# First weights by input block, part of a modulation on TensorE, two matmuls of the last pair moved ahead of its recurrence, four output loads, and a new order of stages, in a two-layer encoder

## The chip, the cores and the metric

The kernel runs on one core of a Trainium2 chip. A core has TensorE (PE in the views; PEld is its loading of weights), VectorE (DVE), ScalarE (ACT), GpSimd (POOL) and SyncE (SP, whose queue issues most DMAs here). Each engine works through its own instructions in order and waits on semaphores for the others. The metric is the device time of one execution in microseconds; lower is better.

## The reference

The input x is 512 tokens of 1024 channels. Two layers, each a mixer and a gated ConvFFN, both as residual blocks with a conditioned RMS norm; then a final norm. The change is in the mixer of layer 0:

```
shift, scale, gate = split(silu(c) @ ada_w[0, 0] + ada_b[0, 0])      # 3 x 1024, one vector
h = rmsnorm(x, norm_g) * (1 + scale) + shift
p = h @ ab_w_in                      # 1024 -> 2560 (hgrn: q, f_fwd, f_bwd, i, g) + r, k, v, wd, ad, gd
y_a = hgrn2(...)                     # 4 heads of 128, both directions, chunks of 32
# rwkv: 8 heads of 64, both directions, in pairs of heads
g = sigmoid(gd) @ g2
for each direction:
    w = -softplus(-(w0 + tanh(wd) @ w2)) - 0.5;  decay = exp(-exp(w));  a = sigmoid(a0 + ad @ a2)
    k_d = k * (1 + (a - 1) * k_a)
    state = state * decay + (state a_t) b_t + v_t k_t;   y += state r_t
    bonus += sum(r * k_d * r_k, per head) * v
y_b = (groupnorm(y) * lnx_w + lnx_b + bonus) * g
x = x + gate * (concat(y_a, y_b) @ ab_w_out)
```

## The kernel before

Activations lie with channels on the 128 partitions and the 512 tokens along the free dimension, so x is eight tiles of 128x512 (an "input block" each). Weights come in blocks of 128x128. Every large product is done in three passes of reduced fp32: a tile is split into a high part (`hi`, by a cast on ACT) and a low part (`lo`, by a subtraction on DVE), and `mm3` issues hi x hi, hi x lo and lo x hi into one PSUM bank. `load_w` loads the blocks of one output block (512 KB for eight inputs) and makes both parts; `gemm` runs `mm3` over the input blocks. PSUM has banks by tag: g, m and c two each, h and o one each.

`start_in` is the first stage. It loads x, takes the norm, and computes shift and scale of this modulation: per input block b a load `ada0` of 1 MB (128 x 2 x 1024) and two dots on DVE (`dot`, L232), each over 1024 columns; then bias (L375), scale (L376) and `modulate` (L171 to L173: nt on DVE, the high half on ACT, the low half on DVE) give the split tile of h. The weights of six output blocks FIRST (k, wd, ad, r, v and gd, in the banks g c g c h o) are loaded one output block after another, 512 KB each, and their 144 matmuls follow.

Then layer 0 proper. Its work is cut into stages: for each of four pairs of rwkv heads `pair` (projections and elementwise preparation), `unit0` and `unit1` (one for each direction: the small triangular solves, a long chain of short DVE instructions at L641 and L643), `inv0` and `inv1` (`rwkv_inverse`, L706 to L735: solve results go through DRAM, loaded as Z and ZT, then TensorE steps at L706, L716, L727 and L733), `chain0` and `chain1` (`rwkv_chain`: a recurrence of 7 steps over chunks, then 16 output matmuls), `post` (`rwkv_post`: group norm, bonus, gate); for each of four hgrn heads `proj` and `hgrn`; and `gate`, `ada` (later modulations) and `out` (early part of the output projection). The list PLAN names each stage, its pair or head, and a number of priority; a scheduler takes from the ready instructions of each engine by priority, so PLAN decides the order in which the engines find the work. `tc.high_priority(...)` raises a piece of code above it.

`rwkv_post` of the last pair is the last work of the mixer: its end normalises the sum of both directions, transposes it, scales it (L781, L784 on ACT), adds the bonus (matmul of `kds` with a block matrix of ones, L788, then DVE L789 and L790) and multiplies by the gate (matmul `lg` x `gd`, L792, then DVE L793). `encoder` then loads the output weights of the two inputs that came last (`ab_out2`, two loads of 512 KB for four output blocks each), multiplies, adds to x (L1179, L334) and forms the next norm (L272). Layer 0's mixer ends at about 622 us of the span; the rest (a ConvFFN, layer 1, a ConvFFN, the final norm) is untouched.

Of the kernel before, what the change touches and what calls it, by code (L numbers as in the profile page):

```python
# [9 lines left out]
F32 = mybir.dt.float32  # L10
F32R = mybir.dt.float32r
# [5 lines left out]
P = 128  # L17
# [21 lines left out]
for _n, _k in COLS:  # L39
# [16 lines left out]
PLAN = [  # L56
    ("pair", 0, 18000), ("proj", 0, -900), ("unit0", 0, 2000), ("unit1", 0, -1000), ("pair", 1, -1000),
# [6 lines left out]
    ("proj", 2, 4500), ("ada", 1, 3200), ("hgrn", 2, 0), ("inv0", 3, 0), ("proj", 3, -5300),  # L64
    ("chain0", 3, 15000), ("inv1", 3, -1500), ("post", 2, 0), ("ada", 2, 1000), ("chain1", 3, 11100),
    ("out", 0, 1400), ("out", 1, -3500), ("hgrn", 3, 14000), ("post", 3, 0),
]
# [3 lines left out]
def encoder(ctx: ExitStack, tc: tile.TileContext, A, out, dbg=None):  # L71
# [272 lines left out]
    def start_in(pool, pool2):  # L344
# [20 lines left out]
        hs, ws = [], {}  # L365
        ps = {i: mps(tag=t) for i, t in zip(FIRST, "gcgcho")}
        for b in range(KB):
            raw = mk(pool, [P, 2, D], "ada", bufs=ADB)
            nc.sync.dma_start(raw, A["ada0"][b])
            if b < len(ps):  # L370
                ws[FIRST[b]] = load_w(A["ab_in"][FIRST[b]], KB, pool2, 2 * len(ps) - 2)
            with tc.high_priority(2 * URGENT):
                for i in range(2):
                    dot(raw[:, i], row, mod[:, b + 8 * i:b + 8 * i + 1])
                dve.tensor_tensor(mod[:, b:b + 9:8], mod[:, b:b + 9:8], col("ada_b", b, 9)[:, ::8], op=ALU.add)  # L375
                dve.scalar_tensor_tensor(gsc[:, b:b + 1], mod[:, 8 + b:9 + b], 1.0, col("norm_g", b), op0=ALU.add, op1=ALU.mult)  # L376
                t = mk(pool, [P, T], "nt", bufs=3)
                hs.append(modulate(t, x[b], rs, gsc[:, b:b + 1], mod[:, b:b + 1]))
        for i in FIRST:
            gemm(ps[i], ws[i], hs, KB)  # L380
        return hs, ps
# [63 lines left out]
    def layer0(ys):  # L445
# [314 lines left out]
        def rwkv_post(q):  # L760
# [17 lines left out]
            for j in range(4):  # L778
# [7 lines left out]
                           scale=col("rwkv_lnx_w", p)[64:128], bias=col("rwkv_lnx_b", p)[64:128])  # L786
            pb = mps(tag="o")
            pe.matmul(pb, bones, kds, start=True, stop=True)  # L788
            dve.tensor_tensor(kds, pb, v, op=ALU.mult)  # L789
            dve.tensor_tensor(y, y, kds, op=ALU.add)  # L790
            pg = mps(tag="o")
            pe.matmul(pg, lg, gd[0], start=True, stop=True)  # L792
            dve.tensor_tensor(y, y, pg, op=ALU.mult)  # L793
# [414 lines left out]
def _layout(inp):  # L1208
# [13 lines left out]
    a["ab_out1"] = np.stack([wo[:, :, list(ks)] for ks in EARLY])  # L1222
    a["ab_out2"] = wo[:, :, list(LATE)].reshape(2, 4, P, 2, P).transpose(0, 2, 1, 3, 4).reshape(2, P, 8, P)
    a["cd_in"] = blocks(f("cd_w_in")[0])[CD_ORDER]
# [45 lines left out]
```

## Time and profile before

| what | us |
| --- | --- |
| median of 3 runs | 1515.57 |
| the runs | 1512.7 to 1520.62 |
| profiled execution | 1522.82 |
| its span | 1521.0 |
| mean granted clock of TensorE in it | 0.944 of full |

Times of the views are those of the profiled execution, counted from the start of its span; the execution is a little longer than the span. A share of busy time is a mean over stages with different limits.

### The profile page before, as it was taken

The page shows a single profiled execution, that of the slowest core. Times are in us where ns is not written, and L with a number is a line of the kernel's source. Part 1 is how long each engine was busy: PE and PEld are TensorE (multiplying, and loading weights), DVE is VectorE, ACT ScalarE, POOL GpSimd, SP SyncE. Part 2 cuts the span into 40 slices and gives each one's busy share as a digit, 9 for nine tenths or more (in the row PEclk, how much of TensorE's full clock was granted, in tenths as well). Part 3 has the DMA queues.
Part 4 walks back from the last instruction along what each step waited for, and adds up shares of the span by engine and source line. Part 5 has one row for each costly group of instructions (what it writes and reads, how often), then busy time and mean ns, then how long its engine had stood idle before and what let it go on. Part 6 is the DMA issues. An engine that isn't in the chain of part 4 may idle for free.

```text
span 1521.0 us, 22382 instructions
## 1 busy us (share of the span) xinstructions
PE 1412.9 (93%) x8446; PEld 1117.7 (73%) x8446; DVE 1028.0 (68%) x2119; ACT 682.8 (45%) x1221; POOL 148.3 (10%) x217
## 2 busy tenths in 40 slices
PE   5997879889998997999999999999999999999997
PEld 3765557566766674788888888887688888888886
DVE  7679776878787864766555795579878654544544
ACT  4454543645544542643233233477465432332343
POOL 1030201102110000000000000039600000000000
PEclk7998688999999996999999999999999999999998
DMA  9221122332252540444644683232133332223221
GB/s 372 74 76 47 50 58 71 102 94 65 65 183 62 177 136 19 165 162 142 202 145 135 227 334 88 96 108 63 35 105 119 117 97 98 94 87 111 94 73 56
DMA packets 77005, 175.08 MB, mean 115 GB/s; under 512 B 28257, under 2 KB 34273, under 8 KB 75873
## 3 DMA queue, kind: packets, MB, share of 16 engines
q1 hardware_dynamic: 76896, 173.65, 35.3%
q8 instruction: 66, 1.08, 0.3%
q14 instruction: 43, 0.34, 0.1%
HBM read 166.80 MB, written 6.82 MB: 114 GB/s over the span
## 4 chain that ended last, share of the span: by engine, by line
PE 72%; DVE 14%; ACT 5%; issue 4%; DMA 3%; POOL 2%; SPq 1%; DVEq 0%; POOLq 0%; ACTq 0%
PE g L144 9%; PE g L146 8%; PE g L145 8%; PE c L145 6%; PE c L144 6%; PE c L146 6%; PE o L144 3%; PE o L145 3%; PE o L146 3%; PE h L144 3%; PE h L146 3%; PE h L145 3%; DVE wlo L139 2%; PE c L733 2%; DVE tt L641 1%
## 5 line engine op out<-in xcount | busy, mean ns | idle before, releaser
L138 ACT CAST whi<-raw 128x512 fp32r<-128x512 f32 (+1 forms) x402 | 242.8, 609 | 520.4 <-PE g L145 204.7
L139 DVE TENSOR_TENSOR wlo<-raw,whi 128x512 fp32r<-128x512 f32 (+1 forms) x402 | 280.5, 703 | 188.7 <-ACT whi L138 185.3
L144 PE MATMUL g<-h,whi 128*128 128x512 f32 x586 | 243.2, 415 | 15.9 <-ACT h L172 5.1
L146 PE MATMUL g<-h,wlo 128*128 128x512 f32 x586 | 237.2, 405 | 4.3 <-DVE wlo L139 4.3
L145 PE MATMUL g<-h,whi 128*128 128x512 f32 x586 | 238.6, 407 | 2.8 <-DVE h L173 2.8
L144 PEld LDWEIGHTS g<-h,whi 128*128 128x128 f32 x586 | 114.3, 195 | 47.5 <-ACT h L172 6.4
L146 PEld LDWEIGHTS g<-h,wlo 128*128 128x128 f32 x586 | 114.3, 195 | 32.6 <-DVE wlo L139 5.9
L145 PEld LDWEIGHTS g<-h,whi 128*128 128x128 f32 x586 | 114.5, 195 | 29.8 <-DVE h L173 4.0
L144 PE MATMUL c<-h,whi 128*128 128x512 f32 x306 | 122.1, 399 | 0.0
L145 PE MATMUL c<-h,whi 128*128 128x512 f32 x306 | 121.2, 396 | 0.0
L146 PE MATMUL c<-h,wlo 128*128 128x512 f32 x306 | 120.6, 394 | 0.0
L1108 POOL TENSOR_TENSOR cpa<-cpa,ta 128x512 f32<-128x512 f32 x51 | 73.5, 1460 | 1.9
L232 DVE SCALAR_TENSOR_TENSOR ra<-ra,row 128x1024 f32<-128x1024 f32 x56 | 67.9, 1218 | 0.0
L144 PEld LDWEIGHTS c<-h,whi 128*128 128x128 f32 x306 | 58.5, 191 | 12.8 <-ACT whi L138 0.3
L145 PEld LDWEIGHTS c<-h,whi 128*128 128x128 f32 x306 | 58.8, 192 | 12.3 <-issue 0.5
L146 PEld LDWEIGHTS c<-h,wlo 128*128 128x128 f32 x306 | 58.5, 191 | 12.0
L641 DVE TENSOR_TENSOR tt<-L,xi 128x60 f32<-128x60 f32 (+24 forms) x248 | 55.7, 225 | 16.7 <-DMA L<-nd 11.3
L643 DVE TENSOR_TENSOR xi<-xi,tt 128x60 f32<-128x60 f32 (+24 forms) x248 | 54.4, 219 | 5.4
L746 ACT COPY X<-c 64x64 f32<-64x64 f32 x56 | 11.7, 208 | 84.0 <-DVE X L745 83.5
L144 PE MATMUL o<-h,whi 128*128 128x512 f32 x122 | 48.1, 394 | 0.8 <-DVE ot L793 0.8
L145 PE MATMUL o<-h,whi 128*128 128x512 f32 x122 | 47.9, 393 | 0.0
L146 PE MATMUL o<-h,wlo 128*128 128x512 f32 x122 | 47.9, 393 | 0.0
(437 smaller groups left out, 2906.5 us busy)
## 6 DMA issues: line engine op xcount, KB each, us to landing
raw<-ffn_up SPq DMA_DIRECT2D x88, 512.0 KB, 3.4
ra<-ada SPq DMA_DIRECT2D x56, 512.0 KB, 4.2
raw<-ab_in SPq DMA_DIRECT2D x35, 512.0 KB, 3.6
raw<-ffn_down SPq DMA_DIRECT2D x32, 448.0 KB, 3.3
raw<-ada SPq DMA_DIRECT2D x24, 512.0 KB, 4.1
ada<-ada SPq DMA_DIRECT2D x8, 1024.0 KB, 10.7
raw<-ffn_down SPq DMA_DIRECT2D x16, 512.0 KB, 3.6
raw<-cd_in SPq DMA_DIRECT2D x12, 512.0 KB, 3.3
```

The lines of the kernel that those rows point to most:

```text
L138: act.copy(hi[:, :n, :], raw[:, k0:k0 + n, :])
L139: dve.tensor_tensor(lo[:, :n, :], raw[:, k0:k0 + n, :], hi[:, :n, :].bitcast(F32), op=ALU.subtract)
L144: pe.matmul(ps, whi, xhi, start=first, stop=False)
L145: pe.matmul(ps, whi, xlo, start=False, stop=False)
L146: pe.matmul(ps, wlo, xhi, start=False, stop=last)
L232: dve.scalar_tensor_tensor(w, w, 1.0, row, op0=ALU.mult, op1=ALU.mult, accum_out=dst)
L641: dve.tensor_tensor(tv, Lv[:, j + 1:, j:j + 1].broadcast_to([P, n, m]), xi[:, j:j + 1, :m].broadcast_to([P, n, m]), op=ALU.mult)
L643: dve.tensor_tensor(xi[:, j + 1:, :m], xi[:, j + 1:, :m], tv, op=ALU.add)
L733: pe.matmul(ps[h][:, c, :], W[hr, c0 + c, :], BRS[hr, c0 + c, :], start=True, stop=True)
L746: act.copy(X[64:128, 1, cn], ps[64:128])
L1108: pl.tensor_tensor(pa, pa, tp, op=ALU.add)
```

## The change

1. **Start.** The modulation of input blocks 0, 1, 3 and 5 (`BY_PE`) is done on TensorE: 32 matmuls of 128x32 with silu(c) as stationary operand, on 64 columns each, then one DVE transpose of 128x64. Blocks 2, 4, 6 and 7 keep the dots. The weights of the six FIRST outputs come by input block (128 x 6 x 128, 384 KB, three buffers) with one cast and one subtraction of 768 columns, and the 18 matmuls of an input block stand right behind its modulation.
2. **Last pair.** The bonus matmul and its multiplication, and the gate matmul with an ACT copy into the space of k, stand ahead of the recurrence of the second direction. `rwkv_post` then only adds and multiplies.
3. **Last output weights.** Four loads of 256 KB (two outputs each); three are issued inside the layer's block of pools, ahead of its end, and none takes the second pool.
4. **PLAN** has a new order and new numbers.

```diff
-    ("pair", 0, 18000), ("proj", 0, -900), ("unit0", 0, 2000), ("unit1", 0, -1000), ("pair", 1, -1000),
+    ("pair", 0, 19000), ("proj", 0, -3500), ("unit0", 0, 5000), ("unit1", 0, -1000), ("inv0", 0, 3000),
...
             raw = mk(pool, [P, 2 * D], "ada", bufs=ADB)
             nc.sync.dma_start(raw, A["ada0"][b])
-            if b < len(ps):
-                ws[FIRST[b]] = load_w(A["ab_in"][FIRST[b]], KB, pool2, 2 * len(ps) - 2)
+            wraw = mk(pool, [P, len(FIRST), P], "wraw", bufs=3)
+            nc.sync.dma_start(wraw, A["ab_first"][b])
             with tc.high_priority(2 * URGENT):
-                for i in range(2):
-                    dot(raw[:, i], row, mod[:, b + 8 * i:b + 8 * i + 1])
-                dve.tensor_tensor(mod[:, b:b + 9:8], mod[:, b:b + 9:8], col("ada_b", b, 9)[:, ::8], op=ALU.add)
+                if b in BY_PE:
+                    v = raw.rearrange("p (k q i) -> p k q i", k=KB, q=4)
+                    pa = mps([P, 64])
+                    for k in range(KB):
+                        for q in range(4):
+                            pe.matmul(pa[32 * q:32 * q + 32, :], sc32[:, k, :], v[:, k, q],
+                                      start=(k == 0), stop=(k == KB - 1), skip_group_check=True)
+                    mt = mk(pool, [P, 64], "mta", bufs=2)
+                    dve.transpose(mt, pa)
+                    new = mt[:, 0:64:32]
+                else:
+                    for i in range(2):
+                        dot(raw[:, i * D:i * D + D], row, mod[:, b + 8 * i:b + 8 * i + 1])
+                    new = mod[:, b:b + 9:8]
+                dve.tensor_tensor(mod[:, b:b + 9:8], new, col("ada_b", b, 9)[:, ::8], op=ALU.add)
...
-        for i in FIRST:
-            gemm(ps[i], ws[i], hs, KB)
+            whi = mk(pool2, [P, len(FIRST), P], "whi", F32R, bufs=5)
+            wlo = mk(pool2, [P, len(FIRST), P], "wlo", F32R, bufs=5)
+            with tc.high_priority(URGENT):
+                act.copy(whi, wraw)
+                dve.tensor_tensor(wlo, wraw, whi.bitcast(F32), op=ALU.subtract)
+            for i, f in enumerate(FIRST):
+                mm3(ps[f], whi[:, i, :], wlo[:, i, :], *hs[b], b == 0, b == KB - 1)
...
         def rwkv_chain(q, u, d):
             SC, X = u["SC"], u["X"]
+            if d == 1 and q["p"] == 3:
+                pb = mps(tag="c")
+                pe.matmul(pb, bones, q["kds"], start=True, stop=True)
+                dve.tensor_tensor(q["kds"], pb, q["v"], op=ALU.mult)
+                pg = mps(tag="c")
+                pe.matmul(pg, q["lg"], gd[0], start=True, stop=True)
+                act.copy(q["k"], pg)
...
-            pb = mps(tag="o")
-            pe.matmul(pb, bones, kds, start=True, stop=True)
-            dve.tensor_tensor(kds, pb, v, op=ALU.mult)
+            if p == 3:
+                pg = q["k"]
+            else:
+                pb = mps(tag="o")
+                pe.matmul(pb, bones, kds, start=True, stop=True)
+                dve.tensor_tensor(kds, pb, v, op=ALU.mult)
+                pg = mps(tag="o")
+                pe.matmul(pg, lg, gd[0], start=True, stop=True)
             dve.tensor_tensor(y, y, kds, op=ALU.add)
-            pg = mps(tag="o")
-            pe.matmul(pg, lg, gd[0], start=True, stop=True)
             dve.tensor_tensor(y, y, pg, op=ALU.mult)
...
         early, yy = layer0(ys)
+        w = []
+        for i in range(3):
+            w += load_w(A["ab_out2"][i], 4)
...
-    w = []
-    for i in range(2):
-        w += load_w(A["ab_out2"][i], KB)
+    w += load_w(A["ab_out2"][3], 4)
```

**Where instructions stand.** A row is a line of the kernel, the operation, the tile that is written and the tiles that are read (with the program's numbers), and the shape. The lines of the changed kernel are its own: `mm3` is L146 to L148 there.

TensorE at the start, before: the first projection matmuls follow the norm's matmuls (L360), for the weights (`whi`, `wlo`) that are there, output by output over the input blocks (`h`).

```order
L360 MATMUL m_183<-sq_205,ones_74 128x512
L144 MATMUL g_211<-h_234,whi_221 128x512
L144 MATMUL c_212<-h_234,whi_243 128x512
L145 MATMUL g_211<-h_235,whi_221 128x512
L146 MATMUL g_211<-h_234,wlo_222 128x512
L145 MATMUL c_212<-h_235,whi_243 128x512
L146 MATMUL c_212<-h_234,wlo_244 128x512
L144 MATMUL g_213<-h_234,whi_265 128x512
L145 MATMUL g_213<-h_235,whi_265 128x512
L146 MATMUL g_213<-h_234,wlo_266 128x512
L144 MATMUL g_211<-h_256,whi_221 128x512
```

No matmul for a modulation stands among them.

The changed kernel at the same stage, around the group of block 3 (L381; `ada_391` is its load), behind both first blocks (`h_328` is block 1):

```order
L147 MATMUL c_214<-h_329,whi_333 128x512
L148 MATMUL c_214<-h_328,wlo_334 128x512
L147 MATMUL h_215<-h_329,whi_333 128x512
L148 MATMUL h_215<-h_328,wlo_334 128x512
L147 MATMUL o_216<-h_329,whi_333 128x512
L148 MATMUL o_216<-h_328,wlo_334 128x512
L381 MATMUL m_395<-ada_391,sc_7_87 32x64 x32
L146 MATMUL g_211<-h_364,whi_369 128x512
L146 MATMUL c_212<-h_364,whi_369 128x512
L147 MATMUL g_211<-h_365,whi_369 128x512
L148 MATMUL g_211<-h_364,wlo_370 128x512
```

The modulation of block 3 stands behind the 36 matmuls of blocks 0 and 1, and block 2 (`h_364`) behind it; that of block 5 stands in the same way behind blocks 2 and 3.

DVE in the changed kernel around its transpose for block 5 (L384), between the work of block 4 (`wlo_475`, low part of its weights) and of blocks 5 and 6:

```order
L173 SCALAR_TENSOR_TENSOR nt_468<-x_34_162,gsc_9_90,rs_208 128x512
L175 SCALAR_TENSOR_TENSOR h_470<-nt_468,mod_8_89,h_469 128x512
L384 STREAM_TRANSPOSE mta_533<-m_500 128x64
L398 TENSOR_TENSOR wlo_475<-wraw_462,whi_474 128x768
L390 TENSOR_TENSOR mod_8_89<-mta_533,cols_69 128x2
L391 SCALAR_TENSOR_TENSOR gsc_9_90<-mod_8_89,cols_69 128x1
L173 SCALAR_TENSOR_TENSOR nt_537<-x_35_164,gsc_9_90,rs_208 128x512
L234 SCALAR_TENSOR_TENSOR ada_565,mod_8_89<-ada_565,row_170 128x1024 x2
L175 SCALAR_TENSOR_TENSOR h_539<-nt_537,mod_8_89,h_538 128x512
L398 TENSOR_TENSOR wlo_544<-wraw_498,whi_543 128x768
```

The transpose waits for TensorE's group of block 5, and block 4's low weights, the dots of block 6 (L234) and all that follows on DVE stand behind it.

TensorE at the end of the last pair, before (L733 is the last inversion, L744 and L752 the recurrence and its outputs, L779 the transposes of `post`):

```order
L744 MATMUL c_5610<-X_4559,sc_4253 64x64 x2
L744 MATMUL c_5615<-X_4559,sc_4253 64x64 x2
L744 MATMUL c_5620<-X_4559,sc_4253 64x64 x2
L752 MATMUL c_5625<-X_4559,sc_4253 64x64 x16
L144 MATMUL c_6239<-h_6156,whi_6221 128x512
L145 MATMUL c_6239<-h_6157,whi_6221 128x512
L146 MATMUL c_6239<-h_6156,wlo_6222 128x512
L779 MATMUL o_6175<-ident_71,ot_6161 128x128 x4
L788 MATMUL o_6183<-kds_4038,bones_106 128x512
L792 MATMUL o_6187<-gd_1471,lg_3859 128x512
L144 MATMUL o_6249<-h_6156,whi_6221 128x512
L145 MATMUL o_6249<-h_6157,whi_6221 128x512
```

The bonus and gate matmuls (L788, L792) stand behind the transposes, and the first matmuls of an output (L144 on bank o) behind them.

In the changed kernel, TensorE at the start of the last recurrence (L753 the inversion, L772 and L780 the recurrence, L807 the transposes):

```order
L753 MATMUL c_5668<-brs_5297,an_4331 128x128 x4
L762 MATMUL c_6042<-kds_3917,bones_106 128x512
L765 MATMUL c_6045<-gd_1745,lg_3792 128x512
L772 MATMUL c_6048<-X_5354,sc_4319 64x64 x2
L772 MATMUL c_6053<-X_5354,sc_4319 64x64 x2
```

The bonus (L762, reading `kds`) and the gate (L765, reading `lg`) are now between the last inversion and the recurrence. The end of the recurrence in the changed kernel and what follows on TensorE:

```order
L772 MATMUL c_6073<-X_5354,sc_4319 64x64 x2
L772 MATMUL c_6078<-X_5354,sc_4319 64x64 x2
L780 MATMUL c_6083<-X_5354,sc_4319 64x64 x16
L146 MATMUL c_6364<-h_6282,whi_6317 128x512
L147 MATMUL c_6364<-h_6283,whi_6317 128x512
L148 MATMUL c_6364<-h_6282,wlo_6318 128x512
L154 MATMUL c_6408<-h_6282,whi_6329 128x256
L155 MATMUL c_6408<-h_6283,whi_6329 128x256
L156 MATMUL c_6408<-h_6282,wlo_6330 128x256
L807 MATMUL o_6301<-ident_71,ot_6287 128x128 x4
L146 MATMUL o_6374<-h_6282,whi_6317 128x512
L147 MATMUL o_6374<-h_6283,whi_6317 128x512
```

L788 and L792 of before are gone from behind the transposes, and three half-width matmuls (L154 to L156) of a later output stand ahead of them.

## Rows read from the trace of the kernel before

**Rows 1.** The page: busy time of each engine, share of the span, instructions.

```profile
PE 1412.9 (93%) x8446; PEld 1117.7 (73%) x8446; DVE 1028.0 (68%) x2119; ACT 682.8 (45%) x1221; POOL 148.3 (10%) x217
```

**Rows 2.** Windows: length, busy (x) PE, PEld, DVE, ACT, POOL, PEclk, DMA, GB/s.

```profile
32.00:36.00 4.00, 4.00 (x10) 3.14 (x11) 4.00 (x10) 1.93 (x4) 0.00 (x0) 0.50 1.02 424
...
36.00:40.00 4.00, 4.00 (x15) 3.16 (x15) 4.00 (x9) 0.72 (x1) 0.00 (x0) 0.78 0.94 392
...
50.00:75.00 25.00, 25.00 (x108) 19.63 (x106) 13.90 (x25) 10.81 (x15) 2.08 (x11) 1.00 0.19 62
```

**Rows 3.** Timeline of DVE, start: start, duration, instruction, [idle before, releaser].

```profile
14.86 1.23 DVE L232 SCALAR_TENSOR_TENSOR ada<-ada,row 128x1024 f32<-128x1024 f32 x1 [1.87 <-DMA ada<-ada]
...
16.01 1.22 DVE L232 SCALAR_TENSOR_TENSOR ada<-ada,row 128x1024 f32<-128x1024 f32 x1
...
17.15 0.68 DVE L139 TENSOR_TENSOR wlo<-raw,whi 128x512 fp32r<-128x512 f32 x1
...
53.05 1.41 DVE L173 SCALAR_TENSOR_TENSOR h<-nt,mod,h 128x512 fp32r<-128x512 f32 x2
```

**Rows 4.** Timeline of PE, start, with the same columns.

```profile
20.25 0.49 PE L144 MATMUL g<-h,whi 128*128 128x512 f32 x1 [4.38 <-ACT h L172]
...
31.71 0.80 PE L145 MATMUL g<-h,whi 128*128 128x512 f32 x1 [1.88 <-DVE h L173]
...
64.39 0.39 PE L146 MATMUL o<-h,wlo 128*128 128x512 f32 x1
```

**Rows 5.** Groups by form, PE, 500:560 us: busy us, mean ns, idle.

```profile
L792 PE MATMUL o<-gd,lg 128*128 128x512 f32 x2 | 1.0, 592 | 0.0
...
L875 PE MATMUL o<-ht,ht 128*32 128x64 f32 x32 | 1.5, 222 | 0.0
```

**Rows 6.** Groups by form, DVE, the whole span.

```profile
L226 DVE STREAM_TRANSPOSE mt<-g 128x256 f32<-128x256 f32 x3 | 1.3, 448 | 1.9 <-PE g L223 1.8
```

**Rows 7.** Waits of PE, 117 to 560 us: first and last of 24 groups.

```profile
PE g L223 <- DMA raw<-ada: 5.1, 4, 2.5
...
PE h L885 <- DVE tt L641: 0.2, 1, 0.2
```

**Rows 8.** Timeline of all engines, 551 to 562 us.

```profile
551.27 0.45 SPq L700 DMA_DIRECT2D ZT<-zd  x1
...
552.58 0.50 PE L145 MATMUL g<-h,whi 128*128 128x512 f32 x1
...
552.91 0.40 PE L146 MATMUL g<-h,wlo 128*128 128x512 f32 x1
...
561.71 0.69 PE L706 MATMUL c<-Z,an 32*32 32x32 f32 x32
```

**Rows 9.** Timeline of all engines, 581.5 to 606 us.

```profile
582.09 0.69 DVE L735 TENSOR_TENSOR sc<-sc,c 128x512 f32<-128x512 f32 x1 [0.57 <-PE c L733]
...
582.83 0.33 PE L744 MATMUL c<-X,sc 128*64 128x64 f32 x2 [0.52 <-DVE sc L735]
...
599.20 0.77 ACT L784 ACTIVATE ot<-o,cols 64x512 f32<-64x512 f32 x1
...
600.02 2.08 PE L788 MATMUL o<-kds,bones 128*128 128x512 f32 x2 [1.65 <-ACT ot L784]
...
602.88 2.08 PE L792 MATMUL o<-gd,lg 128*128 128x512 f32 x2 [0.78 <-DVE kds L789]
...
605.00 0.69 DVE L793 TENSOR_TENSOR ot<-ot,o 128x512 f32<-128x512 f32 x1 [1.37 <-PE o L792]
```

**Rows 10.** Timeline, the last output stage, 607 to 622 us.

```profile
607.26 0.33 SPq L131 DMA_DIRECT2D raw<-ab_out  x1
...
612.35 0.39 PE L152 MATMUL c<-h,whi 128*128 128x256 f32 x1 [0.39 <-ACT whi L138]
...
614.21 0.39 PE L154 MATMUL c<-h,wlo 128*128 128x256 f32 x1 [0.59 <-DVE wlo L139]
...
620.00 2.23 PE L272 MATMUL m<-nsq,ones 128*128 128x512 f32 x6
```

More of the change, by code (lines that the diff above doesn't have):

```diff
@@ L25 @@
 FIRST = (24, 32, 33, 20, 28, 34)
+BY_PE = (0, 1, 3, 5)
 CD_ORDER = [4, 8, 5, 9, 6, 10, 7, 11, 0, 1, 2, 3]
@@ L56 @@
 PLAN = [
-    ("pair", 0, 18000), ("proj", 0, -900), ("unit0", 0, 2000), ("unit1", 0, -1000), ("pair", 1, -1000),
[6 rows of a table removed]
-    ("proj", 2, 4500), ("ada", 1, 3200), ("hgrn", 2, 0), ("inv0", 3, 0), ("proj", 3, -5300),
-    ("chain0", 3, 15000), ("inv1", 3, -1500), ("post", 2, 0), ("ada", 2, 1000), ("chain1", 3, 11100),
-    ("out", 0, 1400), ("out", 1, -3500), ("hgrn", 3, 14000), ("post", 3, 0),
[7 rows of a table added]
+    ("hgrn", 2, -1000), ("ada", 1, -3000), ("proj", 3, -2000), ("unit1", 3, 2000), ("ada", 2, 10000),
+    ("inv0", 3, 12000), ("chain0", 3, 10500), ("inv1", 3, 10000), ("post", 2, 18000), ("out", 0, 7700),
+    ("out", 1, 5000), ("chain1", 3, 8000), ("hgrn", 3, 14500), ("post", 3, -1000),
 ]
@@ L364, in start_in @@
             act.activation(rs, rs, AF.Exp, scale=-0.5)
-        hs, ws = [], {}
+        hs = []
         ps = {i: mps(tag=t) for i, t in zip(FIRST, "gcgcho")}
         for b in range(KB):
-            raw = mk(pool, [P, 2, D], "ada", bufs=ADB)
+            raw = mk(pool, [P, 2 * D], "ada", bufs=ADB)
             nc.sync.dma_start(raw, A["ada0"][b])
-            if b < len(ps):
-                ws[FIRST[b]] = load_w(A["ab_in"][FIRST[b]], KB, pool2, 2 * len(ps) - 2)
+            wraw = mk(pool, [P, len(FIRST), P], "wraw", bufs=3)
+            nc.sync.dma_start(wraw, A["ab_first"][b])
             with tc.high_priority(2 * URGENT):
-                for i in range(2):
-                    dot(raw[:, i], row, mod[:, b + 8 * i:b + 8 * i + 1])
-                dve.tensor_tensor(mod[:, b:b + 9:8], mod[:, b:b + 9:8], col("ada_b", b, 9)[:, ::8], op=ALU.add)
+                if b in BY_PE:
[13 more added lines that the diff above has]
+                dve.tensor_tensor(mod[:, b:b + 9:8], new, col("ada_b", b, 9)[:, ::8], op=ALU.add)
                 dve.scalar_tensor_tensor(gsc[:, b:b + 1], mod[:, 8 + b:9 + b], 1.0, col("norm_g", b), op0=ALU.add, op1=ALU.mult)
@@ L1222, in _layout @@
     a["ab_out1"] = np.stack([wo[:, :, list(ks)] for ks in EARLY])
-    a["ab_out2"] = wo[:, :, list(LATE)].reshape(2, 4, P, 2, P).transpose(0, 2, 1, 3, 4).reshape(2, P, 8, P)
+    a["ab_out2"] = wo[:, :, list(LATE)].reshape(4, 2, P, 2, P).transpose(0, 2, 1, 3, 4).reshape(4, P, 4, P)
     a["cd_in"] = blocks(f("cd_w_in")[0])[CD_ORDER]
@@ L1233, in _layout @@
     w = f("ada_w").reshape(2, 2, KB, P, 3, KB, P)
-    a["ada0"] = w[0, 0, :, :, :2].transpose(3, 4, 2, 0, 1).reshape(KB, P, 2, D)
+    by_pe = w[0, 0, :, :, :2].reshape(KB, P, 2, KB, 4, 32).transpose(3, 1, 0, 4, 2, 5).reshape(KB, P, 2 * D)
+    by_dve = w[0, 0, :, :, :2].transpose(3, 4, 2, 0, 1).reshape(KB, P, 2 * D)
+    a["ada0"] = np.stack([(by_pe if b in BY_PE else by_dve)[b] for b in range(KB)])
+    a["ab_first"] = f("ab_w_in")[0].reshape(KB, P, -1, P)[:, :, list(FIRST)]
     a["ada1"] = np.stack([w[l, s, :, :, ch] for l, s, ch in ADA1]).reshape(3, KB, P, 8, P)
```

12 rows, old and new, of the table PLAN are left out of this document.

## Prediction

> **What bounds the kernel now.** I read the page first. TensorE is busy for 93% of the span, DVE for 68%, ScalarE for 45% [rows 1]. That is a mean over the whole span, most of which (layer 1 and the two feed-forward blocks) the change leaves alone. It works in the first 622 us, so I read that part stage by stage.
>
> The start, by its windows and the timelines of DVE and PE. DVE works without a pause from the first dot (14.86 us) to its last modulate (ends at 53.05 + 1.41 = 54.46 us) [rows 3]. TensorE issues its first projection matmul at 20.25 us, idles for blocks, and issues the last of the six first outputs at 64.39 us [rows 4]. So the first stage is DVE's until about 54 us and TensorE's behind that. Meanwhile the granted clock is 0.50 until 36 us, the lower level (1.2 GHz), and rises to 2.4 GHz within 36:40, behind work that has no gap after 31.71 us [rows 2, 4]; the mean of 0.78 in that window puts the rise at 36 + 4 x (1.00 - 0.78) / 0.50 = 37.8 us. At the lower level ten matmuls take 4.00 us, 0.40 us each; at the full clock 108 take 25.00 us, 0.23 us each [rows 2].
>
> The middle, by the waits of PE in 117 to 560 us: 24 groups, from 5.1 us down to 0.2 us, about 54 us in all [rows 7]. No single wait owns this stretch.
>
> The tail, by the timeline of all engines. The last 128x512 addition into the recurrence's matrices is at 582.09 us, the first recurrence step at 582.83 us, and from ScalarE's last scaling (599.20 + 0.77 = 599.97 us) on everything is serial: bonus matmul 2.08, DVE multiply, DVE add beside the gate matmul 2.08, DVE multiply, split at 605.00 + 0.74 = 605.74 us [rows 9]. The last output stage then waits for weights whose load is issued at 607.26 us: TensorE stands 0.39 us for ScalarE's cast and 0.59 us for DVE's low part [rows 10]. The stage ends with the norm's last matmuls at 620.00 + 2.23 = 622.23 us, 16.5 us behind the split [rows 10].
>
> **The change, part by part.**
>
> *Start, DVE.* Four of the eight input blocks lose two dots each. A dot's step is 16.01 - 14.86 = 1.15 us [rows 3], so 8 go: -9.2 us. Each of the four gains a transpose of 128x64; the 128x256 kind takes 0.45 us [rows 6], so 0.2 to 0.45 us each, +1.2 us. The low parts of the weights cover the same columns (8 x 768 for 12 x 512): none. The sum is -8 us of DVE work.
>
> *Start, TensorE.* It gains four groups of 32 matmuls of 128x32 on 64 columns. The same shape takes 1.5 us for 32 [rows 5]: 1.5 us a group at full clock, 3 us at the lower. The order puts the groups of blocks 3 and 5 behind 36 projection matmuls each, and DVE's work for these blocks waits for them. My hand chain: first projection matmul at 20 us as now, and work without a gap from there, so that I let the clock rise as far behind it as it now does behind 31.71 us, at 26 us; 36 matmuls, 0.40 us each until then and 0.23 us behind it: 31 us. Group of block 3: 32.5. Blocks 2 and 3 (36 x 0.23): 41. Group of block 5: 42.5. From there DVE has, in the order shown, one transpose, three 768-wide low parts (0.9 us each, scaled from 0.68 for 512 [rows 3]) besides that of block 4 (0.9), four dots (4.6), three nt and three low halves (0.7 each), and small ones: 13.5 us, to 56 us. TensorE has 18 matmuls of the last block partly left then (4 to 5 us): end at about 60.5 us against 64.4 us. **-4 us.** Bytes loaded are the same (8 x 1 MB + 6 x 0.5 MB, now 8 x 0.375 MB); loading fills the queues at 424 GB/s until 36 us and thins in 36:40 [rows 2], so arrival does not set the end. Bounds: -8, if TensorE keeps pace with all the DVE work removed; +5, if the clock stays low until the group of block 5.
>
> A rule speaks against the groups. After a group of another tile shape the next 128x512 matmul takes 0.50 us where its neighbour takes 0.40 [rows 8]; some 0.1 to 0.2 us a group, under 1 us for four, within the rounding above. The Trainium skill ("TensorEngine Tiling (Array Packing)", Tiling Modes) says that changing the tiling mode drains TensorE. It gives no price. By that rule with a whole matmul (0.40 us) lost on both sides of each group, the start would give -4 + 3.2 = -1 us. The trace agrees that there is a loss, and has it small.
>
> *Middle.* The table moves whole stages: no instruction is added there but the order. Followed through the whole of both orders, TensorE's accumulated work at each pair's solves, inverses and recurrences is the same to within a few us. I take 0. Below: a third of the 54 us of waits, -18 us. Above: waits grow by a quarter, +13 us. The start's gain goes through if the same stages follow it; behind the six outputs both orders have 24 projection matmuls and then the low-rank products.
>
> *Tail.* The bonus and gate matmuls leave the serial end: it becomes one add and one multiply. From 599.97 to the split takes 2 x 0.7 = 1.45 us in place of 5.77: -4.3 us. Added ahead of the recurrence: the same two, at full clock 1.0 us for two passes [rows 5]; the first runs beside the addition of 582.09 us, whose bank it does not need, the second ends near 584.15, so the recurrence starts at 584.2 and not 582.83: +1.4 us. DVE's multiply (0.69) and ScalarE's copy lie beside the second matmul and the first step. Sum **-3 us**; at the lower clock the two cost 2.08 each and only 1 us is left.
>
> *Output stage.* Three of the four loads are issued before the layer ends, so the halves of outputs 4 and 5 for the first of the two inputs (6 half matmuls) and three whole ones for output 1 are ready ahead of the split. Less behind it: 3 x 0.40 + 6 x 0.12 to 0.20 (half a matmul each, at either level) = 1.9 to 2.4 us; the waits of 0.39 and 0.59 us go [rows 10]; new is a wait for the split's ScalarE half before the first matmul, about 0.7 us by the pass over 512 columns of [rows 3]. Sum -2.2 to -2.7, I take **-2.5 us** (0 if the additions and squares behind it end the stage anyway, -4 at best).
>
> Sum: -4 + 0 - 3 - 2.5 = -9.5 us. The profiled execution took 1522.82 us, 1.8 us more than its span of 1521.0, and 7.3 us more than the median, 1515.57. On it the sum gives 1513.3; against the median, which the result is compared with, 1515.6 - 9.5 = 1506 us.
>
> **Rivals.** The measurement tells about 0.5% (7.6 us) from no change.
>
> *The clock stays low at the start.* In before it rose only at 37.8 us [rows 2]. If small matmuls and waits keep it there too, blocks 0 and 1 end at 20 + 36 x 0.40 = 34.5, the group of block 3 at 37.5, blocks 2 and 3 at 46, the group of block 5 at 47.5, DVE at 61, TensorE at 65.5: +1 us, sum -4.5, 1511 us. For it: TensorE idles ahead of 20 us. Against it: with weights by input block it has work without a gap from there. The Trainium skill ("TensorE: Matmul & The Clock Gate", Part 1: The HAM clock gate) has an idle engine at half rate, and at full rate once it has been busy. By that the rise comes early, as in my chain; the rows of before, with the rise only behind gapless work, agree.
>
> *The start's gain is swallowed.* If some later wait (a solve on DVE, a transfer) fixes the time of the first stages, -4 goes: -5.5, 1510 us. Against it: DVE has slack behind 54 us [rows 3] and TensorE none [rows 2].
>
> *The waits in the middle shrink.* By -18 us at most, half of it as the typical case: 1488 to 1497 us. For it: the waits are there to be had [rows 7]. Against: the totals of both orders agree.
>
> *Slower: the last pair's solve ends too late.* Its result is the input of the last inversion: SP issues the last load of it at 551.27 us, and TensorE first uses it at 561.71 us, so at most 10 us of slack [rows 8]. In the new order some 10 us more DVE work (an estimate, counted over the orders with mean durations) stands ahead of that solve's end, and fewer projection matmuls lie between the inversion's steps. If the solve ends 28 us later, the recurrence starts 18 us later, and with the gains of 9.5 us the result is +8.5 us, 1524 us; from 10 + 9.5 + 7.6 = 27 us on this decides. For it: solves are long chains of short DVE instructions with nothing to shorten them. Against it: so late an end needs twice the work moved.
>
> **Chances.** Forecast (sum between -14 and -7): 0.34. Low clock 0.14, swallowed 0.14 (both within 0.5%). Middle gains more 0.27. Slower 0.11, of which 0.02 end within 0.5% of before. Of the forecast's case 0.02 fall short of 7.6 us. Faster: 0.32 + 0.27 = 0.59, and 0.02 of the swallowed case for a tail at its best: 0.61. Same 0.30. Slower 0.09. The likeliest is 1506 us, by itself 1501.5 to 1508.5; the range is 1489 to 1518, which leaves out half of the slower case and the far end of a middle that gains.
>
> **What would show it.** Right: the last first-stage matmul near 60.5 us, full clock from about 26 us; 8 dots in the first stage, not 16; the two tail matmuls at about 1 us for two passes between the last addition and the recurrence; 1.5 us from ScalarE's scaling to the split; no wait for weights behind it; the last norm matmuls ending near 613 us. Wrong: a PEclk of 0.50 beyond 32 us, a gap on DVE ahead of the transposes of blocks 3 and 5 above 3 us, PE's waits in 117 to 560 us far from 54 us, or the last inversion waiting for its data.

## The result, and the profile after

The changed kernel takes 1501.23 us (median of 4 runs, 1500.19 to 1505.04) against 1518.09 us (4 runs, 1512.7 to 1521.14) in the same comparison. The ratio is 0.9906, 95% interval 0.9881 to 0.9931: faster by 0.7 to 1.2%, some 14 us. A later comparison of the same kernel gave 0.9896. The forecast was 1506 us, ratio 0.994, range 1489 to 1518.

The profiled execution took 1500.64 us, near its median. That of before took 1522.82, which is 6.8 us above 1516 us, the median of 17 later runs in each of two comparisons (a third, of 22 runs, has 1514): by the two traces alone the change looks 22 us strong. I come back to where those 7 us lie.

The start first. The windows (length, busy us with counts of PE, PEld, DVE, ACT, POOL; granted clock, DMA share, GB/s):

```profile
20.00:24.00 4.00, 4.00 (x19) 3.32 (x18) 3.93 (x9) 1.74 (x3) 0.00 (x0) 1.00 1.01 416
24.00:28.00 4.00, 3.94 (x17) 2.90 (x17) 3.22 (x7) 0.68 (x2) 0.00 (x0) 1.00 1.02 416
...
36.00:40.00 4.00, 4.00 (x78) 3.15 (x77) 2.69 (x7) 1.45 (x2) 0.00 (x0) 1.00 1.01 423
```

PEclk is 1.00 (2.4 GHz) throughout, where [rows 2] has 0.50 and 0.78. Timeline of PE (start, duration, instruction, idle before and its releaser):

```profile
19.62 0.50 PE L146 MATMUL g<-h,whi 128*128 128x512 f32 x1 [0.33 <-ACT h L174]
...
28.40 1.10 PE L381 MATMUL m<-ada,sc 128*32 128x64 f32 x64
29.43 0.50 PE L146 MATMUL g<-h,whi 128*128 128x512 f32 x1
29.77 0.40 PE L146 MATMUL c<-h,whi 128*128 128x512 f32 x1
...
37.82 1.10 PE L381 MATMUL m<-ada,sc 128*32 128x64 f32 x64
...
48.98 0.50 PE L146 MATMUL g<-h,whi 128*128 128x512 f32 x1 [1.68 <-ACT h L174]
...
57.20 0.39 PE L148 MATMUL o<-h,wlo 128*128 128x512 f32 x1
```

A group of 32 (64 passes) takes 1.03 us from its start to the next matmul; the first matmul behind it takes 0.50 against 0.40, as in [rows 8]. But the matmul at 48.98 us, behind a wait and no group, takes 0.50 too, so the 0.1 us is not shown to be a price of the group's tile shape. The last first-stage matmul is at 57.20 us, not 64.39 [rows 4]. DVE's last low half of this stage starts at 51.22 us, where it was the pair from 53.05 us [rows 3]; of the four transposes only that of block 5 makes DVE wait:

```profile
38.98 0.25 DVE L384 STREAM_TRANSPOSE mta<-m 128x64 f32<-128x64 f32 x1 [0.45 <-PE m L381]
...
51.22 0.75 DVE L175 SCALAR_TENSOR_TENSOR h<-nt,mod,h 128x512 fp32r<-128x512 f32 x1
```

Which engine sets the end of this stage is read from the chain that ended last, followed back from there. In the kernel before (start, us, what):

```profile
31.00 0.67 DVE h L173
31.71 0.80 PE g L145
32.51 0.43 PE g L146
```

Before, the chain to the last first-stage matmul runs over DVE until 31.67 us and over TensorE alone from there on, with steps of 0.43 us until the clock rises and 0.23 us behind that. In the changed kernel it runs over DVE until 25.3 us, over TensorE from 25.42 to the group of block 5, then over DVE to 48.18, ScalarE's high half, and TensorE again from 48.98.

The tail, timeline of all engines:

```profile
564.22 1.29 DVE L755 TENSOR_TENSOR sc<-sc,c 128x512 f32<-128x512 f32 x2 [1.75 <-PE c L753]
...
564.96 1.12 PE L762 MATMUL c<-kds,bones 128*128 128x512 f32 x2 [0.23 <-DVE sc L755]
565.93 1.02 PE L765 MATMUL c<-gd,lg 128*128 128x512 f32 x2
...
566.88 0.34 PE L772 MATMUL c<-X,sc 128*64 128x64 f32 x4
...
583.04 0.77 ACT L812 ACTIVATE ot<-o,cols 64x512 f32<-64x512 f32 x1
583.85 0.69 DVE L823 TENSOR_TENSOR ot<-ot,kds 128x512 f32<-128x512 f32 x1 [2.80 <-ACT ot L812]
584.57 0.69 DVE L824 TENSOR_TENSOR ot<-ot,k 128x512 f32<-128x512 f32 x1
585.35 0.62 ACT L165 CAST h<-ot 128x512 fp32r<-128x512 f32 x1 [1.54 <-DVE ot L824]
```

From ScalarE's scaling (583.81) to the split (585.35) 1.54 us, where [rows 9] gives 5.8; the recurrence starts 566.88 - 565.51 = 1.37 us behind the last addition, where it was 0.05. Then the output stage, up to the first nt of the feed-forward norm:

```profile
590.68 1.66 ACT L140 CAST whi<-raw 128x512 fp32r<-128x512 f32 x3 [4.71 <-DMA raw<-ffn_up]
...
592.40 0.39 PE L154 MATMUL c<-h,whi 128*128 128x256 f32 x1 [0.38 <-ACT whi L140]
...
593.94 0.39 PE L156 MATMUL c<-h,wlo 128*128 128x256 f32 x1 [0.70 <-DVE wlo L141]
...
606.14 1.28 DVE L316 SCALAR_TENSOR_TENSOR nt<-x,gsc,rs 128x256 f32<-128x256 f32 x3 [1.14 <-ACT rs L305]
```

Both waits of [rows 10] are still there (0.38, 0.70), and ScalarE stands 4.71 us for the first feed-forward weights, with the fourth load's cast and the squares of the norm queued behind. Split to nt takes 20.8 us; before it took 625.77 - 605.77 = 20.0:

```profile
605.77 0.62 ACT L163 CAST h<-ot 128x512 fp32r<-128x512 f32 x1 [5.80 <-DVE ot L793]
...
625.77 0.88 DVE L314 SCALAR_TENSOR_TENSOR nt<-x,gsc,rs 128x256 f32<-128x256 f32 x2 [0.72 <-ACT rs L303]
```

The chain of this stage in the changed kernel (start, us, what) runs over that load, ScalarE's cast and DVE's low part of it:

```profile
586.83 3.60 DMA raw<-ffn_up
...
590.68 0.63 ACT whi L140
...
591.33 0.56 DVE wlo L141
```

From there DVE works without a pause until 602.28 us, on low parts and additions. Before, the chain runs over TensorE's matmuls from 605.74 to 610.8 us.

By the traces: start -7.2, from there to the last addition -10.1 (518.4 to 508.3 us), tail -3.2, output stage +0.8; -19.6 at the first nt (625.77 to 606.14), and 2.5 more in code that did not change.

### The profile page after: what moved, and what is told of

It reads as the page before. It is cut to its first block, busy times and chain, and to the rows that moved or that the text cites. A ratio compares the mean times of both kernels' runs of the same rounds, so it can differ in the third digit from the quotient of the medians.

```text
span 1498.9 us, 22876 instructions
## 1 busy us (share of the span) xinstructions
PE 1410.9 (94%) x8702; PEld 1119.3 (75%) x8702; DVE 1015.2 (68%) x2103; ACT 681.1 (45%) x1217; POOL 150.0 (10%) x217
## 4 chain that ended last, share of the span: by engine, by line
PE 75%; DVE 10%; ACT 5%; DMA 4%; issue 3%; POOL 2%; SPq 1%; DVEq 0%; POOLq 0%; ACTq 0%
PE g L146 9%; PE g L147 9%; PE g L148 9%; PE c L148 6%; PE c L146 6%; PE c L147 6%; PE o L148 3%; PE o L146 3%; PE o L147 3%; PE h L148 3%; PE h L146 3%; PE h L147 3%; PE c L753 2%; POOL cpa L1139 2%; DMA raw<-ada 1%
## 5 line engine op out<-in xcount | busy, mean ns | idle before, releaser
L140 ACT CAST whi<-raw 128x512 fp32r<-128x512 f32 (+1 forms) x390 | 235.4, 607 | 504.9 <-PE g L147 196.2
L141 DVE TENSOR_TENSOR wlo<-raw,whi 128x512 fp32r<-128x512 f32 (+1 forms) x390 | 271.5, 699 | 189.3 <-ACT whi L140 184.6
L146 PE MATMUL g<-h,whi 128*128 128x512 f32 x586 | 241.0, 411 | 6.7 <-ACT h L174 2.0
L148 PE MATMUL g<-h,wlo 128*128 128x512 f32 x586 | 234.6, 401 | 1.5 <-DVE wlo L141 1.5
L147 PE MATMUL g<-h,whi 128*128 128x512 f32 x586 | 233.6, 399 | 0.1
L146 PEld LDWEIGHTS g<-h,whi 128*128 128x128 f32 x586 | 112.5, 192 | 37.2 <-issue 5.1
L148 PEld LDWEIGHTS g<-h,wlo 128*128 128x128 f32 x586 | 112.3, 192 | 28.0 <-DVE wlo L141 2.7
L147 PEld LDWEIGHTS g<-h,whi 128*128 128x128 f32 x586 | 112.7, 192 | 25.3 <-issue 2.2
L146 PE MATMUL c<-h,whi 128*128 128x512 f32 x306 | 121.7, 398 | 0.5 <-ACT h L165 0.5
L148 PE MATMUL c<-h,wlo 128*128 128x512 f32 x306 | 120.9, 395 | 0.0
L234 DVE SCALAR_TENSOR_TENSOR ra<-ra,row 128x1024 f32<-128x1024 f32 x56 | 68.0, 1218 | 1.0 <-DMA ra<-ada 1.0
L146 PEld LDWEIGHTS c<-h,whi 128*128 128x128 f32 x306 | 58.3, 191 | 13.3 <-ACT h L165 1.2
L148 PEld LDWEIGHTS c<-h,wlo 128*128 128x128 f32 x306 | 58.3, 191 | 11.9
L146 PE MATMUL o<-h,whi 128*128 128x512 f32 x122 | 48.2, 395 | 1.6 <-ACT ot L812 1.6
L148 PE MATMUL o<-h,wlo 128*128 128x512 f32 x122 | 48.0, 394 | 0.0
L146 PE MATMUL h<-h,whi 128*128 128x512 f32 x122 | 47.8, 392 | 0.0
```

The lines of the kernel that those rows point to most:

```text
L140: act.copy(hi[:, :n, :], raw[:, k0:k0 + n, :])
L141: dve.tensor_tensor(lo[:, :n, :], raw[:, k0:k0 + n, :], hi[:, :n, :].bitcast(F32), op=ALU.subtract)
L146: pe.matmul(ps, whi, xhi, start=first, stop=False)
L147: pe.matmul(ps, whi, xlo, start=False, stop=False)
L148: pe.matmul(ps, wlo, xhi, start=False, stop=last)
```

## The experiments

The theories named in the expectations: A, the parts add up; B, the middle's gain is chance of one execution; C, the start's gain is swallowed; D, TensorE's idle time brings the clock down at the start, and the groups prevent it; E, the weights by input block alone shorten the start; F and G, the four loads hide nothing, or 2 to 3 us; H, the new list pays only with the new start, since the order is made anew; I, dots or clock cost what the run without groups lost.

The table gives each ratio to the kernel before with its interval, the start of the last first-stage matmul, the middle (from there to the end of the last 128x512 addition), the profiled time less the median of that kernel's runs (above), the middle less that (corrected), and the part of the middle in which TensorE is idle.

```
kernel                       ratio (95%)             first  middle  above   corrected  idle
before (17 later runs)       1                       64.4   518.4   +6.8    511.6      58.5
start alone          e3      0.9965 (0.995, 0.9981)  57.5   521.4   +7.8    513.6      53.5
last pair alone      e5      0.9973 (0.9955, 0.999)  64.0   512.2    0.0    512.2      51.2
four loads alone     e7      0.9978 (0.996, 0.9996)  64.1   515.0   +2.4    512.6      54.2
new list alone       e2      1.0092 (1.0069, 1.0114) 62.5   521.4   -3.7    525.1      53.3
before + filler      e8      1.0006 (0.9989, 1.0023) 64.8   515.9   +4.7    511.2      50.8
after, old list      e1      0.9937 (0.9913, 0.9962) 57.4   519.5   +4.4    515.1      57.9
after, dots only     e4      1.0063 (1.004, 1.0086)  60.9   532.6   +0.5    532.1      56.6
 and old list        e10     1.0089 (1.0062, 1.0116) 60.3   532.8   -4.0    536.8      69.0
after                        0.9906 (0.9881, 0.9931) 57.2   508.3   -0.6    508.9      45.2
after again          e12     0.9896 (0.9874, 0.9918) 57.7   502.3   -2.9    505.2      44.7
after, list nudged   e11     0.9897 (0.9878, 0.9917) 57.3   510.8   +0.7    510.1      55.5
after, two loads     e6      0.9937 (0.9914, 0.9959) 57.5   512.2   +3.1    509.1      44.7
after, fourth apart  e9      0.9948 (0.9928, 0.9967) 57.3   509.1   -3.9    513.0      40.6
```

**The changed kernel with the old list of stages.**

```diff
-    ("pair", 0, 19000), ("proj", 0, -3500),
...
+    ("pair", 0, 18000), ("proj", 0, -900),
...
```

> The changed kernel with the old list of stages; start, last pair and four loads as changed. Theory A (the parts add: start -7 us, order of stages -5 to -10, last pair -3, output stage +1): the order's share goes, so 1506 to 1511 us, ratio 0.993 to 0.997 to the kernel before; the last first-stage matmul stays at 57 us of the span, and PE's waits in the middle come back to about 54 us. Theory B (the order does nothing, the shorter middle is chance of one execution): as the changed kernel, ratio 0.990 to 0.992. Theory C (the start's gain is swallowed, the order brings the rest): ratio 0.997 to 1.000.

0.9937, as A says, and TensorE's idle time in the middle is back at 57.9 us (45.2 in the changed kernel). The order's share is 0.9937 - 0.9906, about 5 us, with intervals that overlap, so B is not excluded by time alone.

**The new list alone**, in the kernel before (the same lines the other way round).

> The kernel before with the new list of stages alone. Theory A: -5 to -10 us, ratio 0.993 to 0.997, with the last first-stage matmul at 64 us as before and PE's waits in the middle near 38 us. Theory B: ratio 0.999 to 1.001. Theory C: -11 us or more, ratio below 0.993.

1.0092: +14 us, which no theory had. TensorE waits 14.3 us in its recurrences for DVE's copies, where the changed kernel has 3.7 (waits of PE, line, releaser, total us, times, longest):

```profile
PE c L744 <- DVE X L745: 14.3, 7, 3.5
```

That this wait costs the 14 us is not shown: TensorE's idle time in the middle is 53.3 us in all, less than the 58.5 of before, and its busy time 468 against 460 us. The two traces differ by 4 us only, since one lies 3.7 us below its median and the other 6.8 above.

**The new start alone** (`start_in` and its layouts put into the kernel before).

> The kernel before with the new start alone. Theory A: the last first-stage matmul at 57 us and not 64, the granted clock 1.00 from 16 to 60 us, the first triangular solve 7 us earlier, and about that at the end: -6 to -7 us, ratio 0.995 to 0.996. Theory B: -9 us or more, ratio below 0.995. Theory C: the first stage ends 7 us earlier, but the end moves by less than 2 us, ratio 0.998 to 1.001.

0.9965: -5.3 us (2.9 to 7.6) of the 7 us by which the first stage ends earlier. The rows are those of A, the time a little short of its 6 to 7 us, whose ratio lies within the interval; C's less than 2 us does not.

**Dots for all eight input blocks**, in the changed kernel.

```diff
-BY_PE = (0, 1, 3, 5)
+BY_PE = ()
```

> The changed kernel with all eight input blocks' modulation by dots on DVE (no groups on TensorE), weights by input block kept. Theory D (the groups fill TensorE between the norm and the first projection, and so hold the clock): TensorE idles from 16 to 20 us again, the granted clock shows 0.50 to 0.6 in 20:28, and DVE has 9 us more work; the last first-stage matmul at 61 to 65 us, +4 to +7 us to the changed kernel, ratio 0.993 to 0.996. Rival E (weights by input block alone make the start short): last first-stage matmul at 57 to 59 us, ratio 0.990 to 0.992.

The first stage is as D says in the main: the window 20:24 has a PEclk of 0.50 (24:28 has 0.83), and the last matmul is at 60.92 us, 3.7 us behind the changed kernel and 3.5 ahead of before.

```profile
20.00:24.00 4.00, 3.56 (x8) 2.81 (x9) 4.00 (x8) 1.94 (x3) 0.00 (x0) 0.50 1.02 424
```

So the weights by input block bring half of the start's gain and the groups the other half. The chain of this run stays on DVE until 50.1 us and goes over TensorE only from there: the groups pay by the dots that they take from DVE, and the low clock at 20 us lay beside the chain. But the kernel is slower than before, 26 us behind the changed one, and 24 us of them arise in the middle.

**The last pair's two matmuls alone.**

> The kernel before with the last pair's bonus and gate alone ahead of the recurrence. Theory A (the serial end shrinks): from the last addition into the matrices to the first recurrence step 2.0 us in place of 0.74, from ScalarE's last scaling to the split 1.5 us in place of 5.8, -3 us in all, ratio 0.997 to 0.999. Rival: the two matmuls fall to the lower clock (2.08 us each), only -1 us, ratio 0.999 to 1.000.

0.9973. The rows are those of theory A: scaling ends at 592.99 + 0.77, split at 595.30 us.

```profile
592.99 0.77 ACT L792 ACTIVATE ot<-o,cols 64x512 f32<-64x512 f32 x1
595.30 0.62 ACT L163 CAST h<-ot 128x512 fp32r<-128x512 f32 x1 [1.54 <-DVE ot L804]
```

**Two loads in the changed kernel, and four loads in the kernel before.** (The lines of the diff of the last output weights, undone or done alone.)

> The changed kernel with the last output weights in two loads, as before. Theory F (the four loads only put another wait in the place of the old one, ScalarE now stands behind the first feed-forward load): from the split to the first nt of the feed-forward norm 20 us, where the changed kernel has 20.8 and the kernel before 20.0; ratio 0.990 to 0.991. Rival G (the four loads hide 2 to 3 us): 22 to 23 us, +2 us to the changed kernel, ratio 0.9915 to 0.993.

> The kernel before with the last output weights in four loads alone. Theory F: from the split to the first nt of the feed-forward norm 20.5 to 21 us, where the kernel before has 20.0: +0.5 to +1 us, ratio 0.999 to 1.002. Rival G (they hide 2 to 3 us): 17 to 18 us, ratio 0.997 to 0.999.

Split to nt: 19.9 us with two loads in the changed kernel (589.44 to 609.33), 0.9 less than with four; 19.8 us with four loads in the kernel before (601.80 to 621.58), 0.2 less than with two, where F had 0.5 to 1 more. In this stage the loads are worth a microsecond or less, and G's 2 to 3 us are not there. With two loads ScalarE waits for `ab_out` where it waits for `ffn_up` with four:

```profile
594.63 1.66 ACT L140 CAST whi<-raw 128x512 fp32r<-128x512 f32 x3 [4.57 <-DMA raw<-ab_out]
```

The run times say more than the stage. With four loads both pairs are faster: by 3.3 us (0.6 to 6.1) in the kernel before, which is G's ratio, and by 0.9937 - 0.9906, about 5 us, in the changed one, which was not timed beside that run. From the first nt to the end of the span, in code that did not change, the six traces with two loads have 892.2 to 896.9 us (mean 894.9) and the eight with four 891.5 to 895.0 (mean 892.8). So the loads may save some 2 us behind the stage; by which path, no run shows.

**A filled gap.** Four matmuls whose result nobody uses, between the norm and the first projection of the kernel before; all other instructions of TensorE and DVE from the first pair on stand in the same order.

```diff
+        fill = mps()
+        for i in range(4):
+            pe.matmul(fill, ones, sq, start=True, stop=True)
```

> The kernel before with four extra matmuls (128x512, results unused) on TensorE between the norm's matmuls and the first projection; every other instruction stays in its place. Theory D (the clock falls because TensorE idles there): granted clock 1.00 or nearly so from 16 to 40 us where it was 0.50 to 0.78, the last first-stage matmul at 60 to 62 us in place of 64.4, -3 us, ratio 0.997 to 0.999. Rival: the waits of 0.7 to 1.9 us for input blocks behind it bring the clock down anyway, 0.50 by 28 us, the last matmul within 1 us of 64.4, ratio 0.999 to 1.001.

The rival is right. Windows as above:

```profile
20.00:24.00 4.00, 2.11 (x6) 1.04 (x6) 4.00 (x8) 1.74 (x4) 0.00 (x0) 1.00 1.02 426
24.00:28.00 4.00, 2.09 (x4) 0.77 (x3) 4.00 (x11) 1.23 (x3) 0.00 (x0) 0.58 1.00 419
28.00:32.00 4.00, 1.65 (x3) 0.83 (x3) 4.00 (x8) 1.10 (x2) 0.00 (x0) 0.50 1.02 423
32.00:36.00 4.00, 3.86 (x9) 3.09 (x10) 4.00 (x10) 2.35 (x5) 0.00 (x0) 0.50 1.02 428
```

The clock stays up to 24 us and falls while TensorE, half idle, waits for blocks; the last matmul is at 64.83 us. Until 32.1 us the chain runs over DVE, busy for 4.00 of every 4 us: so far the low clock is a mark of DVE's pace, not a cost. From 32.14 us on TensorE works without a gap, as from 31.71 in the kernel before, and some 14 of its matmuls still take 0.43 us and not 0.23. The filler did not reach that part. At most 2.8 us (14 x 0.20, an estimate from these rows) could be had there; no run shows whether they can.

**The fourth load's parts in the other pool**, so that its cast stands ahead of the feed-forward weights'.

```diff
-    w += load_w(A["ab_out2"][3], 4)
+    w += load_w(A["ab_out2"][3], 4, w2pool, 3)
+    spools.append(spools.pop(0))
```

> The changed kernel with the split parts of the fourth output load in the other pool, so that its cast stands ahead of the first feed-forward weights on ScalarE. Theory F: TensorE's waits of 0.38 us (for that cast) and 0.70 us (for its low part) go, split to first nt 19 to 19.8 us in place of 20.8, -1 to -1.5 us to the changed kernel, ratio 0.9885 to 0.990. Rival: additions, squares and the norm's table load set that stage, 20.5 to 21 us, ratio 0.990 to 0.991.

The rival: 20.4 us (586.26 to 606.65). The cast moves up (587.68) and ScalarE then stands for the feed-forward weights as before, ahead of the squares, and the chain of the stage runs over that load, its cast and DVE's low part as in the changed kernel:

```profile
587.68 0.62 ACT L140 CAST whi<-raw 128x512 fp32r<-128x512 f32 x1 [0.80 <-DVE h L166]
591.40 1.14 ACT L140 CAST whi<-raw 128x512 fp32r<-128x512 f32 x2 [3.11 <-DMA raw<-ffn_up]
```

Its median is 5 us above the changed kernel's with the same order in the middle. The cause is open; the changed kernel was not timed beside this run.

**Dots and the old list; the list nudged; the changed kernel again.**

```diff
-BY_PE = (0, 1, 3, 5)
+BY_PE = ()
...
-    ("pair", 0, 19000), ("proj", 0, -3500),
...
+    ("pair", 0, 18000), ("proj", 0, -900),
...
```

> The changed kernel with dots for all eight input blocks and with the old list of stages (the run without TensorE's groups had the new list). Theory H (the new list of stages pays only with the new start, because the order that comes of it is made anew when the start changes): the first stage ends at 61 us as it did there, but the middle is as long as with the old list elsewhere (about 519 us from the last first-stage matmul to the first recurrence step of the last pair, where the run with the new list had 534), so -6 to -8 us to the kernel before, ratio 0.994 to 0.997. Rival I (the dots themselves, or the lower clock at the start, cost the 26 us there): ratio 1.004 to 1.009 as there.

```diff
-("pair", 1, -1000)
+("pair", 1, -900)
```

> The changed kernel with one number of its list of stages moved by 100 (the second pair's, -1000 to -900), which puts 8% of TensorE's and 22% of DVE's instructions between the first pair and the last recurrence out of place. Theory H: the gain of the list hangs on that very order, and some of it goes, +3 to +10 us to the changed kernel, ratio 0.993 to 0.998. Rival: the order is worth little in itself, ratio 0.989 to 0.992.

> The changed kernel unaltered, on the chip of these runs. Both theories: ratio 0.988 to 0.993. If the granted clock in the stretch where DVE sets the pace (110 to 220 us) falls at other points than in its first execution, the time moves by some us with the same order.

H's two forecasts fail. The dots lose as much with the old list, and a nudge that puts about a fifth of DVE's instructions out of place loses nothing (in its trace TensorE is idle for 10 us more of the middle and busy for 8 us less, at a granted clock of 0.92 against 0.91). In the run with dots and the old list the third triangular solve starts at 213.98 us, behind a wait of 7.49 us for its input, where the old list with the new start has 207.02 and 2.54 (DVE's timeline, one row of each):

```profile
213.98 0.31 DVE L661 TENSOR_TENSOR tt<-L,xi 128x31 f32<-128x31 f32 x1 [7.49 <-DMA L<-nd]
```

```profile
207.02 0.21 DVE L661 TENSOR_TENSOR tt<-L,xi 128x31 f32<-128x31 f32 x1 [2.54 <-DMA L<-nd]
```

Between these two kernels, with one list, about 30% of DVE's instructions of the middle are out of place. That the order costs the 13 us there (22 corrected), and not the dots, is therefore likely, but not shown: no run held the order and changed the start.

## Why the prediction came out as it did

**Start, -4: too small; the chain of the changed kernel was right, the reading of before was not.** Measured -7.2 us at the last first-stage matmul. Two terms of the chain were too dear: the clock (I let it be low until 26 us; it never fell, since TensorE goes from the norm's matmuls at 15.7 us into the first groups) and the groups (1.5 us; 1.03). The 32 of [rows 5] counts passes, two for a matmul, of which a group has 64: by that row a group was 3 us, and that 1.5 lay nearer was luck. The group of block 3 came at 28.4 and not at 31 us, that of block 5 at 37.8 and not at 41; DVE's last low half ended at 52 and not at 56 us. The chain behind that, 4 to 5 us of TensorE, held (5.2). Two readings of before were wrong. Its first stage was DVE's until 31.7 us and not until 54: behind that TensorE had 132 matmuls without a gap, a backlog that the weights by input block cut (with them and all dots TensorE's part starts at 50.1 us). And its clock was not 0.50 from the start on, but 1.00 in 16:20, with no matmul, and fell behind 20 us:

```profile
16.00:20.00 4.00, 0.00 (x0) 0.00 (x0) 3.88 (x10) 2.88 (x5) 0.00 (x0) 1.00 1.01 424
```

The rival with the low clock is out. Of its premise the run with the filler settles one half: until 32 us there was no time in the low clock; behind that it stays open. The Trainium skill ("TensorE: Matmul & The Clock Gate", Part 1: The HAM clock gate) has an idle engine at half rate and a busy one at full rate; the granted clocks of the two kernels agree with a lag: in before 1.00 in 16:20 with no matmul, and 0.50 in 32:36 with TensorE busy for 4.00 of 4 us [rows 2]; 1.00 throughout in the changed kernel. Whether a low clock costs anything depends on the engine that sets the pace.

**The start's gain swallowed: no.** Alone it is worth 5.3 us (2.9 to 7.6) at the end.

**Middle, 0: wrong, the rival "the waits shrink" holds.** TensorE's waits from the last first-stage matmul to the last addition fall from 57 us in 25 groups to 44 us in 27, and its busy time hardly changes (the middle of before, and of the changed kernel):

```profile
64.40:582.80 518.40, 459.89 (x4054) 335.40 (x4052) 398.25 (x1064) 259.34 (x498) 63.06 (x129) 0.90 0.30 89
```

```profile
57.20:565.50 508.30, 463.13 (x4057) 337.86 (x4055) 395.91 (x1067) 258.80 (x500) 63.54 (x129) 0.91 0.31 91
```

This is not chance of one execution: four traces with the order of before (before, e5, e7, e8) have 51 to 59 us of idle time, four with the changed order (after, e12, e6, e9) 41 to 45. But of the 10 us of time in the two traces more than half is chance: the three other kernels with the order of before have 512 to 516 us there, and the excess of each profiled execution over its median explains the rest. Corrected, the order of before has 511 to 513 us (mean 512), the changed one 505 to 513 (mean 509). That leaves about -3 us, and e1 gives 5 by time. The step that failed is "TensorE's accumulated work at each pair's solves, inverses and recurrences is the same", taken as 0: its busy time in the whole middle is the same within 3 us, but its idle time was not in the count. Which of DVE's instructions in front of a solve or a copy make the difference, no run shows. The rival on the other side (a solve over 27 us late) did not come: in the changed kernel no inversion waits for Z. With the new list and the old start one does, for 3.4 us, in a kernel that is 14 us slower.

**Tail, -3: right.** 5.80 to 1.54 at the end is -4.26, the later recurrence +1.32, the recurrence itself -0.2: -3.2 us. Alone 0.9973, 4 us with an interval of 1.5 to 7.

**Output stage, -2.5: wrong.** Measured +0.8 up to the first nt. I counted TensorE's work and the weights it waits for, and left out ScalarE's and DVE's order: the first feed-forward weights' cast stands in front of the fourth load's cast and of the squares, their low parts stand in front of the additions, and both wait for a load that is issued at 586.83 us, right behind the split's low half (ends at 586.69). TensorE's part left the chain, and this one took its place at nearly the same length. The wait did not go, it changed its name (4.71 us on ScalarE). The prediction had this case, additions and squares that end the stage anyway, at 0. Time that the loads may save behind the stage was in no term.

**The sum.** -7 for -4, -3 to -5 for 0, -3 for -3, +1 for -2.5: -12 to -14 us for -9.5, where -14 was measured. The total came close because two errors leaned against a third; that is luck.

## What to carry to other kernels

A moved transfer or cast is priced on the queue that has to process it: read what stands in front of it and behind it there, not only who waits for it now. Before a difference of two traces is explained, compare each profiled time with the median of its kernel's runs, and look for the stretch in which kernels with the same order differ; here that was worth 7 of 22 us. A low clock on an engine that waits for another is a symptom: follow the chain that ended last, and count the clock as a cost only where the chain runs over that engine.

## What the runs showed that I had not expected

The same order of instructions does not give the same middle: 512.2 to 518.4 us in kernels with over 98% of the middle's instructions in the order of before, and 508.3 and 502.3 us for two executions of the changed kernel. One place where it shows is 180:185, at much the same point of the order, before and with the last pair's edit alone:

```profile
180.00:185.00 5.00, 5.00 (x26) 3.56 (x25) 1.99 (x7) 0.00 (x0) 0.00 (x0) 0.50 0.00 0
```

```profile
180.00:185.00 5.00, 3.93 (x34) 2.94 (x34) 3.90 (x14) 0.41 (x2) 0.00 (x0) 0.85 0.00 0
```

In one execution TensorE gets 0.50 there and is busy for all of it, in the other 0.85 and gets more done in less. Where the clock falls is not fixed by the order alone.

And the parts do not add: start, last pair, loads and list alone give -5.3, -4.1, -3.3 and +14 us, which sums to +1; in one kernel they give -14. The first three do add within their intervals: -12.7 alone, -9.6 (-6 to -13) together with the old list. The list of stages is worth +14 us with the old start and about -5 with the new one.
